# A four-layer trunk on one core: the first S5 recurrence in a written order on all engines, with its phases in the first step and its operators built on VectorE

## The chip, the core and the metric

The kernel runs on one core of one Trainium2 chip. A core has a matrix engine (TensorE, "PE" in the profile, its weight loads "PEld"), a vector engine (VectorE, "DVE"), a scalar engine for activations (ScalarE, "ACT"), a general engine (GpSimd, "POOL") and a sync engine that issues DMAs (SyncE, "SP"). Each engine runs its own instructions in their order; semaphores tie the engines together. The metric is the device time of one launch in microseconds (us), lower is better. Before the change it is 2361.99 us, the median of three runs (2357.68 to 2366.71).

## What is computed

The reference runs 512 tokens of width 1024 through four layers: S5, gated linear attention, differential attention, S5; each mixer is followed by a SwiGLU block. Only the first S5 mixer matters here. Cut down, it is

```python
h = rmsnorm(x, norm_mix[0])
dt = exp(log_dt);  ab = exp((lam_re + 1j * lam_im) * dt)   # 64 groups x 64 states
bb = (ab - 1) / lam * b                                    # 64 states x 16 channels for each group
s[t] = ab * s[t - 1] + bb @ h[t]                           # for each group, 512 tokens
y = real(c @ s) + d_skip * h
z = gelu(y)
a, g = split(z @ w_glu);  x = x + a * sigmoid(g)
```

All arithmetic is in float32; large products use three passes with operands split into a rounded high part and a rest.

## The kernel before

The mixer takes four tokens at a time: 128 blocks of four tokens, and 64 groups as 32 pairs, so that a pair of groups fills 128 partitions (2 x 64 states, or 2 x 4 x 16 inputs). Eight steps kk = 0 to 7 each treat four pairs, that is 128 channels. Two steps share one "half" h = kk // 2 of eight pairs, for which the operators are made together.

For one step the work is as follows; the names are those of `s5_pipe` (L1267) and `s5_first` (L1397).

- `up` (L1295, L1303): PE turns four 128x128 tiles of the normed input `hu` (it lies in the tile `scr`), and ACT copies them to `room`, the step's input U.
- `states` (L1305): PE forms V, two banks of 128x512, as input operator (`in`) times U (L1311). DVE turns V by the phases `cs` (cosine and sine) with four products into `mods` (L1313 to L1316); an addition and a subtraction follow (L1318, L1319), on POOL in the first S5 and on DVE in the second one.
- `scans` (L1321): two scans along time on DVE with the decay `r4` (L1328, L1330), then four products with `cs` into `prods` (L1329, L1331 to L1333).
- `outputs` (L1335): PE sums U times `map` and the four `prods` times `out` into the bank `y` (L1340, L1342), ACT applies gelu (L1344).
- `turned` (L1350): PE turns the result back (`zp`, L1353); ACT rounds it into `zT` (L488) and DVE takes the rest (L489).
- `glu` (L1358): 12 products of 128x512 into four banks `acc` (L370 to L372), the second half of the GLU's columns. Their weights come by `staged` (L334, the tile `wst`), `high` (ACT, L346) and `low` (DVE, L350).

The first S5 also makes its operators while it runs (`steps` and `ins` in `s5_first`):

- X (the input operator's powers): `s5_x` with twelve DVE products and sums of `cross` (L1017 to L1019) for each half, in two parts of 9 and 3; `s5_xt` turns X on PE (`xps`, L1143), ACT copies it in (L1153).
- Q (the output operator's powers): `s5_qt` turns C on PE (`cps`, L1057), ACT places it (L1075), and six products and sums of 128x512 follow (L1017 to L1019 with tile Q), all on POOL.
- the map of four tokens onto four: `s5_rows` on PE (`rps`, L1110), DVE and ACT put it into `rsb` (L1120, L1124), and `s5_map` sends it through DRAM: one DMA out (L1126) and eight in (L1135).
- pads: DMAs copy Q into `out` and X's base into `bpad` (L1100).
- phases: `s5_phases_first` (L980) forms the phase of 128 time blocks with two small products (`rough`, L987, L988), takes whole turns off on ACT (L990, L992), forms the angle with three products (L994 to L996), clips it on DVE (L998), and takes sine, absolute value and cosine on ACT (L999 to L1001). It is called once per step, one step ahead, and fills the decay (L1003, L1004) as well.

Before all this stand `s5_small`, a long chain of DVE instructions on 128x64 tiles that makes decay, phase and scale out of the parameters, and `s5_in`, which normalizes x: squares on ACT (L470), the power -1/2 on POOL (L459), and scale and gain for two tiles on ACT and POOL (L477, L479) and for two on DVE (L481).

In this region the order of all five engines' instructions is what a scheduler makes of the program. The loop is laid out one step deeper than the data needs: step kk's turn runs `states(kk)`, `scans(kk-1)`, `outputs(kk-2)`, `turned(kk-2)`, `glu(kk-3)`. After the pipeline, `s5_glu` runs the rest of the GLU: the gates of the finished columns on ACT (L1548), then three more sets of 96 products of 128x512.

Of the kernel before, what the change touches and what calls it, by code (L numbers as in the profile page):

```python
# [11 lines left out]
F32 = mybir.dt.float32  # L12
# [256 lines left out]
class Trunk:  # L269
# [558 lines left out]
    def sincos(self, pool, sn, cs, r, n, tag):  # L828
# [6 lines left out]
        with self.tc.high_priority(offset=60):  # L835
            nc.scalar.activation(sn, r, AF.Sin)
            nc.scalar.activation(cs, a[:], AF.Sin, scale=-1.0, bias=self.halfpi[:])


    def s5_small(self, pool):  # L840
# [6 lines left out]
        nc.scalar.activation(warm[:], self.halfpi[:], AF.Sin)  # L847
        self.magic = cp.tile([P, 1], F32, name="magic")
# [5 lines left out]
        if True:  # L854
# [5 lines left out]
            draw = p.tile([16, P], F32, name="draw")  # L860
            nc.sync.dma_start(draw[:], i["s5_d"].rearrange("l (k p) -> (l k) p", p=P))
# [6 lines left out]
            nc.tensor.transpose(ps[:, 3, :16], draw[:], self.ident[:16, :16])  # L868
# [10 lines left out]
            v.tensor_copy(self.dcol[:], ps[:, 3, :16])  # L879
# [58 lines left out]
        p = Slices(self.wp.tile([P, 2048], F32, tag="whl", name="params2", bufs=5))  # L938
        self.s5_rows_of_phases(p, pool, keep["fhi"], keep["flo"], keep["f"])
# [3 lines left out]
    def s5_rows_of_phases(self, p, cp, fhi, flo, f):  # L943
# [4 lines left out]
        v = nc.vector  # L948
        part = p.tile([P, 96], F32, name="rowparts").rearrange("p (k z b) -> p k z b", z=3, b=4)
# [6 lines left out]
        nc.scalar.copy(hi[:], lo)  # L956
        v.tensor_copy(rest, hi[:].bitcast(F32))
        v.tensor_tensor(lo, lo, rest, op=ALU.subtract)
        self.frow = cp.tile([12, 8, P], F32R, name="frow")
        for q in range(2):  # L960
            ps = self.tp("frow")
            for j in range(4):
                nc.tensor.transpose(ps[:12, j], part[:, 4 * q + j].rearrange("p z b -> p (z b)"), self.ident[:])
            nc.scalar.copy(self.frow[:, 4 * q : 4 * q + 4], ps[:12])
# [9 lines left out]
        nc.scalar.mul(self.nident[:], self.ident[:], -1.0)  # L974
# [3 lines left out]
    def s5_phases_first(self, pool, kk, cs, r4):  # L978


        nc = self.nc
        mm = nc.tensor.matmul
        flat = lambda y: y[:].rearrange("p a b -> p (a b)")
        row = self.frow[:, kk]
        fine, rest = (self.counts[:, z].rearrange("p a b -> p (a b)") for z in range(2))
        rough = flat(self.tp("rough"))
        mm(rough, row, fine, start=True, stop=False)  # L987
        mm(rough, row, rest, start=False, stop=True)  # L988
        k = pool.tile([P, 512], F32, tag="turns", name="turns")
        nc.scalar.activation(k[:], rough, AF.Identity, bias=self.magic[:])  # L990
        kr = pool.tile([P, 512], F32R, tag="turnsr", name="turnsr")
        nc.scalar.activation(kr[:], k[:], AF.Identity, bias=self.mmagic[:])  # L992
        g = flat(self.tp("angle"))
        mm(g, row, fine, start=True, stop=False)  # L994
        mm(g, self.nident[:], kr[:], start=False, stop=False)
        mm(g, row, rest, start=False, stop=True)  # L996
        ca = k[:]
        nc.vector.tensor_scalar(ca, g, -0.5, 0.5, op0=ALU.max, op1=ALU.min)  # L998
        nc.scalar.activation(cs[:, 1], ca, AF.Sin, scale=self.two_pi)  # L999
        nc.scalar.activation(ca, ca, AF.Abs)  # L1000
        nc.scalar.activation(cs[:, 0], ca, AF.Sin, scale=-self.two_pi, bias=self.halfpi[:])  # L1001
        r4 = r4.rearrange("p (b m) -> p b m", m=P)
        nc.scalar.copy(r4, self.k5["r4"][:, 4 * kk : 4 * kk + 4].unsqueeze(2).broadcast_to([P, 4, P]))  # L1003
        nc.gpsimd.memset(r4[:, :, 0:1], 0.0)  # L1004
# [1188 lines left out]
```

## Time and profile before

| quantity | us |
|---|---|
| median of three runs | 2361.99 |
| the profiled execution, its own time | 2366.1 |
| span of the profile, first to last instruction | 2364.4 |
| PE busy in the span | 2245.8 (95%) |
| DVE, ACT, POOL busy in the span | 1586.0, 1119.2, 332.3 |
| first DVE instruction of the recurrence (L1313) | at 48.63 |
| first GLU gate behind the recurrence (L1548) | at 201.68 |

A row of the page's timeline gives start, duration, engine, line, operation, output<-input, shape and count, and in brackets how long the engine stood idle before it and whose completion ended the wait. A row of the group view gives count, total and mean time, and the idle time before. A row of the windows view gives, for one stretch, the busy time of every engine with its number of instructions, the granted TensorE clock (1.00 is full), the share of time that the DMA engines were busy, and GB/s. Successive instructions of one engine overlap a little, so the distance from start to start is shorter than the duration.

### The profile page before, as it was taken

The numbers are of one execution on the slowest core, as the hardware profiler recorded it, in microseconds if no ns is written. First come the engines' busy times: TensorE is split into PE (matmuls) and PEld (weight loads), VectorE is DVE, ScalarE is ACT, GpSimd is POOL, SyncE is SP. The second block draws the span as 40 slices with busy tenths as digits, with TensorE's granted clock in tenths as the row PEclk, the third lists the DMA queues.
The fourth block names the chain that finished last, engine by engine and source line by source line (L and its number), as shares of the span: only waits on it lengthen the run. The fifth ranks groups of instructions, "written<-read, shape, count | busy, mean of one in ns | idle before, by whom it ended". The sixth has DMA issues, their size and how long they took to land. (4 is left out here: it accounts for less than half of the span.)

```text
span 2364.4 us, 37216 instructions
## 1 busy us (share of the span) xinstructions
PE 2245.8 (95%) x14847; PEld 1985.6 (84%) x14847; DVE 1586.0 (67%) x2416; ACT 1119.2 (47%) x1790; POOL 332.3 (14%) x417
## 2 busy tenths in 40 slices
PE   4799989999999999999999998999999799999997
PEld 3577888898977789898987787989999688989996
DVE  7765587876833468786753566886856864967674
ACT  3454454554552346555544575653534233634442
POOL 3330123324000011111001231111000100101000
PEclk9699999999999999999999999999999899999999
DMA  4114676676332268576344564895742545766631
GB/s 111 32 39 142 160 186 155 165 178 156 86 104 72 79 144 212 146 181 177 108 140 116 115 134 122 209 240 127 187 98 81 121 130 151 176 175 157 162 77 67
DMA packets 291719, 320.17 MB, mean 135 GB/s; under 512 B 68005, under 2 KB 231097, under 8 KB 291290
## 3 DMA queue, kind: packets, MB, share of 16 engines
q1 hardware_dynamic: 229434, 236.57, 33.4%
q0 software_dynamic: 62112, 81.22, 18.7%
q8 instruction: 117, 1.92, 0.3%
q14 instruction: 56, 0.46, 0.1%
HBM read 285.88 MB, written 16.65 MB: 128 GB/s over the span
## 5 line engine op out<-in xcount | busy, mean ns | idle before, releaser
L350 DVE TENSOR_TENSOR whl<-wst,whl 128x1024 fp32r<-128x1024 f32 x272 | 332.1, 1223 | 310.2 <-ACT whl L346 309.6
L346 ACT CAST whl<-wst 128x1024 fp32r<-128x1024 f32 x272 | 285.2, 1050 | 383.2 <-PE acc L372 265.5
L535 PE MATMUL a<-side,whl 128*128 128x256 f32 x3168 | 388.7, 280 | 9.0 <-ACT whl L346 5.9
L535 PEld LDWEIGHTS a<-side,whl 128*128 128x128 f32 x3168 | 375.9, 191 | 11.0 <-ACT whl L346 7.1
L370 PE MATMUL acc<-whl,act 128*128 128x512 f32 x704 | 278.2, 395 | 3.0 <-DVE g L580 3.0
L371 PE MATMUL acc<-whl,act 128*128 128x512 f32 x704 | 275.0, 391 | 0.0
L372 PE MATMUL acc<-whl,act 128*128 128x512 f32 x704 | 274.7, 390 | 0.0
L535 PE MATMUL c<-side,whl 128*128 128x256 f32 x2112 | 255.8, 278 | 4.3 <-DVE whl L350 4.3
L535 PEld LDWEIGHTS c<-side,whl 128*128 128x128 f32 x2112 | 248.6, 189 | 4.7 <-DVE whl L350 4.7
L350 DVE TENSOR_TENSOR whl<-slot,whl 128x1024 fp32r<-128x1024 f32 x105 | 127.9, 1223 | 66.4 <-ACT whl L346 65.9
L370 PEld LDWEIGHTS acc<-whl,act 128*128 128x128 f32 x704 | 132.1, 188 | 33.2 <-DVE g L580 4.2
L372 PEld LDWEIGHTS acc<-whl,act 128*128 128x128 f32 x704 | 132.2, 188 | 28.0
L371 PEld LDWEIGHTS acc<-whl,act 128*128 128x128 f32 x704 | 132.2, 188 | 25.9 <-issue 0.2
L370 PE MATMUL acc<-whl,hT 128*128 128x512 f32 x352 | 143.4, 407 | 2.1 <-DVE ro L1918 1.5
L346 ACT CAST whl<-slot 128x1024 fp32r<-128x1024 f32 x105 | 110.0, 1052 | 73.9 <-PE acc L372 28.2
L371 PE MATMUL acc<-whl,hT 128*128 128x512 f32 x352 | 138.4, 393 | 1.0 <-DVE whl L350 1.0
L372 PE MATMUL acc<-whl,hT 128*128 128x512 f32 x352 | 138.5, 394 | 0.0
L535 PE MATMUL a<-sides,whl 128*128 128x256 f32 x1056 | 134.0, 283 | 1.6 <-DVE x L518 1.6
L535 PE MATMUL d<-sides,whl 128*128 128x256 f32 x1056 | 133.5, 283 | 1.3 <-ACT whl L346 1.3
L535 PEld LDWEIGHTS a<-sides,whl 128*128 128x128 f32 x1056 | 129.4, 191 | 2.7 <-issue 2.0
L535 PEld LDWEIGHTS d<-sides,whl 128*128 128x128 f32 x1056 | 128.9, 191 | 2.0 <-ACT whl L346 1.9
L571 POOL DMA_DIRECT2D wst<-in_ffn_w_gate_up_dram x44 | 56.8, 1290 | 445.7 <-DMA wst<-in_ffn_w_gate_up_dram 257.1
(442 smaller groups left out, 3994.7 us busy)
## 6 DMA issues: line engine op xcount, KB each, us to landing
wst<-in_ffn_w_gate_up_dram SPq DMA_DIRECT2D x88, 512.0 KB, 4.5
wst<-in_ffn_w_down_dram SPq DMA_DIRECT2D x88, 512.0 KB, 4.6
slot<-in_ffn_w_gate_up_dram SPq DMA_DIRECT2D x69, 512.0 KB, 5.4
wst<-in_ffn_w_gate_up_dram POOLq DMA_DIRECT2D x44, 512.0 KB, 6.3
halves<-in_ffn_w_gate_up_dram SPq DMA_DIRECT2D x42, 512.0 KB, 6.2
wst<-in_s_w_glu_dram SPq DMA_DIRECT2D x32, 512.0 KB, 3.9
wst<-in_gla_w_in_dram SPq DMA_DIRECT2D x24, 512.0 KB, 3.7
wst<-in_diff_w_qkv_dram SPq DMA_DIRECT2D x24, 512.0 KB, 3.8
```

The lines of the kernel that those rows point to most:

```text
L346: self.last["high"] = self.nc.scalar.copy(hl[:, 0], w[:])
L350: self.last["low"] = self.nc.vector.tensor_tensor(hl[:, 1], w[:], hl[:, 0].bitcast(F32), op=ALU.subtract)
L370: mm(out, lh, rh, start=first, stop=False)
L371: mm(out, lh, rl, start=False, stop=False)
L372: self.last["mm"] = mm(out, ll, rh, start=False, stop=last)
L535: mm(o, hl[:, x, k, c], side[:, y, k], start=first and not (j or k or n), stop=k == 3 and n == 2, skip_group_check=True,)
L571: nc.gpsimd.dma_start(w[:], left.quarter(*plus, b), accum_op=ALU.add)
```

## The change

The change rewrites the order of the first S5 by hand and moves some of its work.

1. `s5_pipe` gets `before` and `hooks`. With hooks, all five engines take the program's order as written (`hand_all`), and the loop is one step shallower: `states(kk)`, `outputs(kk-1)`, `up(kk+2)`, `products(kk+1)`, `turned(kk-1)`, scans and turns of kk, `rest(kk-1)`, `glu(kk-2)`. `products` (the PE part of the former `states`) is now one step ahead of the DVE part; `split_t` is taken apart into `turned` (ACT) and `rest` (DVE).
2. The addition and the subtraction in `states` run on DVE in both S5.
3. Q is made by DVE instead of POOL: in odd steps Q, in even steps X. X's first part is split into a base (`pre`) and `one`.
4. Phases are made early: those of steps 0 and 1 ahead of or in the start, 2 to 5 started in step 0, 6 and 7 in step 1 (sines in step 3). Their banks come from `acc` instead of `tp`; `cs` gets five places, the decay its own tile (`s5_decays`).
5. The input gain goes into the input operator: `bb` is multiplied by the gain, laid out by group with two DMAs, instead of x; d_skip gets the gain as well. `s5_in` then only scales by ACT; the eps is added on ACT too. The input operator has two buffers, and one `xps` bank holds both its parts.
6. The GLU's weights are fetched once per even step at its end, rounded (ACT) at the start of the next even step, and the rest is taken (DVE) right behind its `states`.
7. In the start, the two sine instructions on ACT come ahead of the squares of x (`issue_after`).

The core of the diff:

```diff
+        if hooks:
+            hook = lambda name, kk: hooks[name](kk) if name in hooks else None
+            self.hand_all()
+            before(up, products)
+            for kk in range(10):
+                hook("first", kk)
+                if kk % 2 == 0 and kk:
+                    hls[kk // 2 - 1] = self.high(stage[kk // 2 - 1], 2, 512)
+                hook("operators", kk)
+                if kk < 8:
+                    states(kk)
+                if kk % 2 == 0 and kk:
+                    self.low(hls[kk // 2 - 1], stage[kk // 2 - 1])
+                hook("behind states", kk)
+                if 1 <= kk < 9:
+                    outputs(kk - 1)
+                if kk + 2 < 8:
+                    up(kk + 2)
+                if kk + 1 < 8:
+                    products(kk + 1)
+                hook("behind products", kk)
+                if 1 <= kk < 9:
+                    turned(kk - 1)
+                hook("behind zp", kk)
+                if kk < 8:
+                    scan(kk, 0)
+                    scan(kk, 1)
+                    hook("behind scans", kk)
+                    for k in range(4):
+                        turn(kk, k)
+                hook("beside", kk)
+                if 1 <= kk < 9:
+                    rest(kk - 1)
+                hook("beside 2", kk)
+                if kk % 2 == 0 and kk < 8:
+                    stage[kk // 2] = self.staged(self.wb_src(wg, kk, D), 2, 512)
+                if kk >= 2:
+                    glu(kk - 2)
+                hook("last", kk)
+            self.hand()
+            return accs
...
+            def before(up, products):
+                phases((0, "rough"))
+                up(0)
+                ins(0)
+                phases((0, "angle"), (0, "clip"), (0, "sines"))
+                new_x(1)
+                products(0)
+                phases((1, "rough"))
+                decays(0)
+                up(1)
+                phases((1, "angle"))
+                out_pads(0)
+                out_pads(1)
+                raw[2] = self.s5_loads(p, 0, 16, 8, 2)
...
+            def operators(kk):
+                if kk + 1 < 8:
+                    ins(kk + 1)
+                    decays(kk + 1)
+                if kk % 2 and kk < 7:
+                    new_q(kk // 2 + 1)
+                if kk % 2 == 0 and kk < 8:
+                    rv[kk // 2] = self.s5_rows(8, bp, Q[kk // 2][0])
...
+            def behind_products(kk):
+                if kk == 0:
+                    phases((1, "clip"), (2, "rough"), (1, "sines"))
+                    rows[1]()
+                    phases((2, "angle"), (3, "rough"))
+                if kk % 2 == 0 and 2 <= kk < 7:
+                    out_pads(kk + 1)
...
+            def behind_scans(kk):
+                if kk == 0:
+                    phases((2, "clip"), (2, "sines"), (3, "angle"))
...
+            def beside(kk):
                 h = kk // 2
+                if kk == 0:
+                    X[1][2]()
+                    phases((3, "clip"), (4, "rough"), (3, "sines"), (4, "angle"))
+                elif kk % 2 == 0 and h + 1 < 4:
+                    new_x(h + 1)
+                elif kk % 2 and kk < 7:
+                    Q[h + 1][2]()
+
+            def beside_2(kk):
+                h = kk // 2
+                if kk % 2 == 0 and kk < 6:
+                    if kk:
                         X[h + 1][2]()
+                    X[h + 1][3]()
+                    self.s5_b_pads(bp, X[h + 1][0])
+                if kk == 0:
+                    phases((4, "clip"), (5, "rough"), (4, "sines"), (5, "angle"))
+                if kk == 1:
+                    phases((6, "rough"), (6, "angle"), (6, "clip"), (7, "rough"))
+                if kk % 2 and kk < 7:
+                    Q[h + 1][3]()
+                    out_pads(kk + 1)
...
+        def pre():
+            if gain is not None:
+                g = gain[:, b0 : b0 + nb].unsqueeze(1).broadcast_to([P, 2, nb, 16])
+                eng.tensor_tensor(bb[:], bb[:], g, op=ALU.mult)
             f(0, 0, X[:, 0, :, 0], bb[:, 0], bb[:, 1], ALU.subtract)
             f(0, 0, X[:, 1, :, 0], bb[:, 1], bb[:, 0], ALU.add)
```

In step 1, `behind_states` clips and takes the sines of step 5; in step 2, `first` forms the angle of step 7 and `behind_states` clips it and starts the map (as in each even step); in step 3, `behind_zp` takes the sines of steps 6 and 7. From the end of the recurrence on, each engine's instructions are the same as before and in the same order.

More of the change, by code (lines that the diff above doesn't have):

```diff
@@ L993, in s5_phases_first @@
[L993 to L1001, printed above, removed]
@@ L1002, in s5_phases_first, with rough @@
-        r4 = r4.rearrange("p (b m) -> p b m", m=P)
-        nc.scalar.copy(r4, self.k5["r4"][:, 4 * kk : 4 * kk + 4].unsqueeze(2).broadcast_to([P, 4, P]))
-        nc.gpsimd.memset(r4[:, :, 0:1], 0.0)
+        k = self.np_.tile([P, 512], F32, tag="h", name="turns")
+        at = {}
+        def rough():
+            p = self.acc("rough")[:]
+            mm(p, row, fine, start=True, stop=False)
+            mm(p, row, rest, start=False, stop=True)
+            nc.scalar.activation(k[:], p, AF.Identity, bias=self.magic[:])
+            at["kr"] = kr = self.np_.tile([P, 512], F32R, tag="hh", name="turnsr", bufs=2)
+            nc.scalar.activation(kr[:], k[:], AF.Identity, bias=self.mmagic[:])
@@ L1474, in s5_first @@
+            rv = {}
+            hooks = {
+                "first": first, "operators": operators, "behind states": behind_states, "behind zp": behind_zp,
+                "behind products": behind_products, "behind scans": behind_scans, "beside": beside, "beside 2": beside_2,
+            }
+            accs = self.s5_pipe(0, hu, zT, True, room, get, before, hooks)
         self.x = self.xp.tile([P, NT, D], F32, tag="x", name="x")
```

317 lines of the change are left out of this document (196 added, 121 removed).

## The prediction

> **What bounds the kernel now.** I read the windows first, cut at the two ends of the recurrence, then the groups of POOL and DVE inside it, then the same recurrence in the second S5 as a timeline.
>
> ```profile
> 48.60:201.70 153.10, 131.26 (x1019) 105.31 (x1019) 102.82 (x134) 75.15 (x125) 51.50 (x45) 0.83 0.24 52
> 201.70:272.20 70.50, 70.50 (x326) 58.27 (x324) 29.36 (x36) 25.01 (x40) 5.12 (x4) 1.00 0.62 171
> ...
> 201.68 2.67 ACT L1548 ACTIVATE gate<-acc 128x512 f32<-128x512 f32 x4 [1.82 <-PE acc L372]
> ```
>
> The columns are PE, PEld, DVE, ACT, POOL busy, then the granted clock. From 201.7 on PE is busy 70.50 of 70.50 us at full clock, and its later order is unchanged, so whatever the change gains must be gained before that gate. In the 153.1 us before it no engine is full: DVE 102.8, ACT 75.2, POOL 51.5, PE 131.3 at a mean clock of 0.83. That is about 131.3 x 0.83 = 109 us of full-clock work, 13.6 a step, in steps that take 153.1/8 = 19.1. The engines wait for each other.
>
> ```profile
> L1319 POOL TENSOR_TENSOR mods<-mods 128x512 f32<-128x512 f32 x8 | 14.6, 1820 | 2.4 <-DVE mods L1316 2.4
> L1019 POOL TENSOR_TENSOR Q<-Q,dq 128x512 f32<-128x512 f32 x8 | 12.2, 1524 | 0.3
> ...
> L1328 DVE TENSOR_TENSOR_SCAN mods<-cs,mods 128x512 f32<-128x512 f32 x8 | 12.6, 1573 | 1.2 <-POOL mods L1318 1.2
> ```
>
> A POOL pass over 128x512 takes 1.5 to 1.8 us, and the scan on DVE beside it 1.57 in the mean. The second S5 has no such POOL work:
>
> ```profile
> 1904.70 0.69 DVE L1313 TENSOR_TENSOR mods<-V,cs 128x512 f32<-128x512 f32 x1
> ...
> 1908.29 1.23 DVE L1328 TENSOR_TENSOR_SCAN mods<-cs,mods 128x512 f32<-128x512 f32 x1
> ...
> 1910.54 0.67 DVE L1329 TENSOR_TENSOR prods<-mods,cs 128x508 f32<-128x508 f32 x1
> ...
> 1912.91 0.69 DVE L489 TENSOR_TENSOR zT<-zp,zT 128x512 fp32r<-128x512 f32 x1
> 1914.12 1.23 DVE L350 TENSOR_TENSOR whl<-wst,whl 128x1024 fp32r<-128x1024 f32 x1 [0.51 <-ACT whl L346]
> 1915.26 0.68 DVE L1313 TENSOR_TENSOR mods<-V,cs 128x512 f32<-128x512 f32 x1
> ```
>
> Here a scan is 1.2, and DVE runs without gaps: six passes for `states` in 1908.29 - 1904.70 = 3.59, two scans in 2.25, four turns in 2.37, low 1.14. A plain pass is 0.60 from start to start. These are the prices of the written order.
>
> **The start.** In before, six rows set it:
>
> ```profile
> 16.10 1.06 ACT L470 ACTIVATE sq<-xin 128x1024 f32<-128x1024 f32 x1 [8.82 <-DMA xin<-in_x_dram]
> 17.28 0.15 DVE L457 TENSOR_SCALAR ms<-ms 128x1 f32<-128x1 f32 x1 [1.99 <-ACT sq L470]
> 18.58 1.13 ACT L477 ACTIVATE sq<-xin,rs 128x1024 f32<-128x1024 f32 x1
> 19.89 2.34 DVE L904 TENSOR_TENSOR params<-params 128x64 f32<-128x64 f32 x1
> ...
> 46.48 3.75 PE L1311 MATMUL V<-room 128*128 128x128 f32 x16 [0.24 <-ACT room L1303]
> ...
> 48.63 0.69 DVE L1313 TENSOR_TENSOR mods<-V,cs 128x512 f32<-128x512 f32 x1 [4.18 <-PE V L1311]
> ```
>
> DVE's parameter chain loses 2.0 us at 17.28 and 2.1 at 19.89 (a 0.2 us instruction that took 2.34 beside POOL's gain product); both causes go. The gain product on `bb` and the split of `dcol` add about 1. So X of half 0 is ready some 3 us earlier. The normed input no longer passes through DVE and POOL: from x's arrival (16.1; the gain's two DMAs of 64-byte pieces now lie ahead of it, I take 16.8) ACT does four squares, four small additions, four scalings, two small copies: 4 x 1.25 + 4 x 0.2 + 4 x 1.13 + 0.8 = 11.1, done at 28.0. Then `rough`, `up`, `xps`, `angle` and V follow on PE at the slow rate of the 46.48 row (3.75 for V), back to back from 28.4 to 37.3, with clip and sines beside V. `states(0)` starts at about 36.7: 12 us ahead of 48.63.
>
> **Steps 0 and 1.** What is added here is the phases of steps 2 to 7. ACT carries them:
>
> ```profile
> L1001 ACT ACTIVATE cs<-turns,halfpi 128x512 f32<-128x512 f32 x8 | 5.8, 723 | 0.1
> L992 ACT ACTIVATE turnsr<-turns,mmagic 128x512 fp32r<-128x512 f32 x8 | 5.8, 722 | 0.3
> L990 ACT ACTIVATE turns<-rough,magic 128x512 f32<-128x512 f32 x8 | 5.5, 687 | 3.1 <-PE rough L988 2.7
> ...
> L999 ACT ACTIVATE cs<-turns 128x512 f32<-128x512 f32 x8 | 5.0, 631 | 7.0 <-DVE turns L998 7.0
> L1000 ACT ACTIVATE turns<-turns 128x512 f32<-128x512 f32 x8 | 5.0, 628 | 0.0
> ...
> 41.34 0.80 PE L995 MATMUL angle<-turnsr,nident 128*128 128x512 f32 x1
> 42.06 0.79 PE L996 MATMUL angle<-counts,frow 12*128 12x512 f32 x1
> ```
>
> A phase costs ACT 1.4 for the turns and 2.0 for the sines, and PE five products of 0.72 at the slow rate, half of that at full clock. Queued on ACT in step 0: the turns of step 1, seven copies of about 0.6, four times 3.4, in all 19.5. That gives 56 if PE always delivers; at full clock the `rough`-after-`angle` chain adds 4 (60.5), at half clock 11 (67.7). In step 1 the path to `states(2)` runs over y(0) on PE, gelu, V, `zp` and the copy to `zT` on ACT, `rest(0)` on DVE, the turns and angle of step 6, its clip, and the second half of Q, because DVE's order puts them in that row: 15 us at full clock (PE 8, five ACT passes 4, DVE 3), about 21 at half. So `states(2)` starts between 75.5 and 88.3. I take 84: the phases' products, of which four in five use 12 of 128 rows, are what PE does in step 0, so the clock will mostly be low. So the head start is spent here, on phases that before still had to make in its later steps.
>
> **Steps 2 to 7** are then bound by DVE. Its other prices:
>
> ```profile
> 28.08 0.55 DVE L1017 TENSOR_TENSOR X<-X,pw 128x384 f32<-128x384 f32 x1
> 28.55 0.55 DVE L1019 TENSOR_TENSOR X<-X,dx 128x384 f32<-128x384 f32 x1
> ...
> 92.64 0.28 DVE L1018 TENSOR_TENSOR dx<-bb,s5fi 128x128 f32<-128x128 f32 x1
> 92.84 0.28 DVE L1017 TENSOR_TENSOR X<-bb,s5fr 128x128 f32<-128x128 f32 x1
> ...
> 166.08 0.36 DVE L1120 SCALAR_TENSOR_TENSOR rsb<-mask,dcol,rps 128x16 f32<-128x16 f32 x2
> ...
> 183.21 1.07 DVE L489 TENSOR_TENSOR zT<-zp,zT 128x512 fp32r<-128x512 f32 x1
> 184.19 2.35 DVE L350 TENSOR_TENSOR whl<-wst,whl 128x1024 fp32r<-128x1024 f32 x2
> ```
>
> Q's six passes on DVE are not in the trace: 0.47 for 128x384 here is the low end, POOL's 1.5 the high one. I take 0.60, the plain pass of the same size. Gain 0.33, base 6 x 0.2, X 6 x 0.47, rest 1.0. An even step: 3.6 + 1.14 + 0.36 + 2.25 + 2.37 + 1.53 + 1.0 + 2.82 = 15.1 (step 2 has one clip more, 15.7; step 6 has no X, 10.7). An odd step: 3.6 + 2.25 + 2.37 + 1.0 + 3.6 = 12.8. Steps 2 to 6 are 15.7 + 12.8 + 15.1 + 12.8 + 10.7 = 67.1. PE's 13.6 a step falls to about 12 without the phases and lies beside it, if at full clock; ACT has 5 to 6. The new waits of the written order: on DVE `rest(kk-1)` stands ahead of the second part of X or Q and waits for ACT's copy to `zT`, whose chain (y 4.5, gelu, V, `zp`, copy) ends 9 to 10 us into a step at full clock, while DVE gets there at 10 to 12; with PE at half clock it is some 6 late, and then X or Q, `rps`, the map and the next y are late with it. On PE `rps` waits for the end of Q with y behind it; y ends there 5.4 into the step, early enough. On SP the GLU's weights and the next norm's gain (it waits for zp(6)) queue behind pads and maps; they are needed 11 and 22 us later and cost nothing while the queue runs. The decay's own tile, the joint `xps` bank and the eps on ACT lie under DVE's row and cost nothing either; uncovered they would cost their ACT time, under 1 us a step.
>
> **The tail.** y(6) needs the last map, made in step 6 at 5.2 and sent through DRAM:
>
> ```profile
> 132.84 0.57 SPq L1126 DMA_DIRECT2D rd<-rsb  x1
> 134.87 3.65 SPq L1135 DMA_DIRECT2D scr<-rd  x8
> ...
> scr<-rd SPq DMA_DIRECT2D x32, 32.0 KB, 2.0
> ...
> 166.68 0.38 PE L1340 MATMUL y<-scr,room 128*128 128x128 f32 x2
> 171.14 1.95 PE L1311 MATMUL V<-room 128*128 128x128 f32 x16
> ```
>
> From DVE's row to landing: 0.6 to the issue, 2.0, 3.7 for eight issues on SP, 2.0: 8.3. So y(6) starts at 13.5 of step 6, 2.8 into step 7. Behind it in PE's order: y 4.5, gelu and `zp` 1.5, glu(5) 2.7, y(7) 4.5, gelu and `zp` 1.4, glu(6) and glu(7) 2.7 each: 22.8 after the start of step 7. (y is 171.14 - 166.68 = 4.46; twelve GLU products are at most 70.50/24 = 2.9 by the second window, which holds three sets of 96 and some transposes.)
>
> **The clock.** Three windows of 3.4 us in before:
>
> ```profile
> 142.40:145.80 3.40, 3.40 (x9) 2.08 (x9) 3.40 (x3) 2.95 (x5) 1.85 (x1) 0.61 0.00 1
> 145.80:149.20 3.40, 3.40 (x13) 2.52 (x12) 1.34 (x2) 0.38 (x2) 0.00 (x0) 0.50 0.02 5
> 149.20:152.60 3.40, 3.40 (x17) 3.40 (x17) 0.00 (x0) 3.35 (x5) 0.10 (x1) 0.50 0.00 0
> ```
>
> PE was busy throughout, and the clock stayed at half for three windows. One such episode costs PE 5 us, of which about 2 fit into a step's slack: I add one, 3. The Trainium skill's page "TensorE: Matmul & The Clock Gate" (Part 1: The HAM clock gate) says that the full clock comes back after about one busy window of 3.4 us; these rows disagree. By it the low clock would be short, `states(2)` would start near 75.5, and the time would be the third rival's.
>
> **The sum.** 84 + 67.1 + 22.8 + 3 = 177 for the end of glu(7). In before it lies 2.0 behind the first gate, at 203.7. The gain is 26.7, and the profiled execution's 2366.1 becomes 2339.4. The median of the runs shown is 4.1 below that execution: 2335.
>
> **The rivals.** (1) Slower: the half clock holds through the DVE-bound steps, because each leaves PE gaps of 2 to 3 us. A step is then PE's, 2 x 12 = 24 instead of 14. Steps 2 to 7 and the tail from 88.3: 88.3 + 5 x 24 + 2 x 19 = 246, 43 us later than before: 2405. It decides from about three such steps on (3 x 10 eats the 27). For it: 0.50 in the rows above; against it: those spells ended while PE was dense, and a PE-bound step is dense. 5%. (2) The phases do not overlap: turns, angle, clip and sines run in turn, 1.4 + 1.5 + 0.7 + 2.0 + 1.3 = 6.9 for each of five. `states(2)` starts near 99, the end is 192, the gain 11: 2350, no change that can be told. For it: PE and ACT pass every phase to and fro twice; against: the order puts another phase's sines into each wait. 9%. (3) PE at full clock from step 0 on and no episode: 75.5 + 67.1 + 22.8 = 165.4, gain 38: 2324. 20%. (4) DVE's new passes cost more: Q at 1.05 (between its bounds) is 24 x 0.45 = 11 more, or SP's map chain is late by 3 in each even step: 2345. 13%. The forecast keeps 53%.
>
> **How the numbers follow.** About 0.5%, 12 us, is what a measurement of this kernel can tell from no change. Forecast, (3) and (4) are faster, 86%; (2) and the edge of (4) same, 8%; (1) and the unforeseen slower, 6%. The range runs from (3) with a start 8 us better to rival (2): 2316 to 2351.
>
> **What would show it.** `states(0)` near 37; ACT nearly full between 40 and 62; a distance of two steps near 28 from step 2 on, with DVE above 9 tenths; no POOL pass over 128x512; the first gate near 175. Wrong would be a granted clock of 0.5 over several of the later steps, or DVE waiting for PE's V or ACT's zT there.

## The result and the profile after

The changed kernel takes 2345.73 us (median of 5 runs, 2341.71 to 2348.9) where the kernel before takes 2359.25 (5 runs, 2355.8 to 2366.71): a ratio of 0.9938, 95% interval 0.9916 to 0.9959. That is 13.5 us less, half of what was forecast. The forecast went from 2361.99, the median of the three runs known then; with five runs the median of before is 2.7 lower. The profiled execution of the changed kernel has an own time of 2344.99 and a span of 2343.3.

In the new kernel's lines the six passes of `states` are L1384 to L1389, the scans L1393, the turns L1402 and L1406, `y` L1413 and L1415, gelu L1417, `zp` L1430, ACT's copy to `zT` L1431 and DVE's rest L1435. The map's rows are L1156 and L1160, its DMAs L1162 and L1171. The weights' load is L336, their rounding and low part L346 and L350 as before, the reload of x L1689, the gate L1763. Where an experiment adds lines, the later numbers shift by as many.

First the busy row of the page after:

```profile
PE 2234.0 (95%) x14847; PEld 1981.7 (85%) x14847; DVE 1594.0 (68%) x2461; ACT 1114.6 (48%) x1769; POOL 275.6 (12%) x378
```

POOL has lost 57 us and DVE gained only 8. Next the windows of after, cut at the starts of steps 0, 1, 2 and 7 on DVE and at the first gate, with steps 3 and 6 singly, and then the same cut of before; the columns are those of the forecast.

```profile
36.35:57.90 21.55, 16.94 (x118) 11.02 (x116) 14.18 (x26) 15.22 (x25) 0.21 (x2) 0.75 0.39 75
57.90:78.45 20.55, 16.79 (x125) 13.08 (x123) 14.38 (x23) 14.48 (x24) 0.10 (x1) 0.75 0.04 8
78.45:153.99 75.54, 67.04 (x666) 60.19 (x666) 68.41 (x115) 31.07 (x51) 0.53 (x5) 0.91 0.24 50
...
96.37:109.92 13.55, 13.15 (x142) 11.85 (x142) 13.08 (x21) 7.89 (x14) 0.11 (x1) 1.00 0.21 52
...
143.36:153.99 10.63, 10.20 (x103) 9.39 (x102) 10.63 (x18) 3.61 (x6) 0.11 (x1) 1.00 0.14 29
153.99:182.73 28.74, 21.21 (x118) 19.13 (x118) 16.30 (x20) 8.02 (x10) 0.97 (x1) 0.82 0.75 253
```

```profile
48.63:172.30 123.67, 105.25 (x838) 82.36 (x838) 83.52 (x113) 64.41 (x112) 47.58 (x42) 0.79 0.19 37
172.30:201.68 29.38, 25.96 (x184) 22.91 (x183) 19.30 (x21) 10.72 (x13) 3.89 (x3) 1.00 0.47 119
```

The first gate comes 201.68 - 182.73 = 19.0 us earlier. Of these, 48.63 - 36.35 = 12.3 are the earlier start, 123.67 - (21.55 + 20.55 + 75.54) = 6.0 come from the way from `states(0)` to `states(7)`, and the tail, 28.74 against 29.38, gives almost nothing.

Most of the earlier start is the normed input. Its last tile came from DVE in before, behind a power on POOL (first row), and comes from ACT now (second row):

```profile
35.69 1.28 DVE L481 SCALAR_TENSOR_TENSOR scr<-xin,rs,gain 128x1024 f32<-128x1024 f32 x1 [0.46 <-POOL rs L459]
```

```profile
26.64 1.15 ACT L1318 ACTIVATE scr<-xin,rs 128x1024 f32<-128x1024 f32 x1
```

It is ready 9.2 us earlier (27.8 instead of 37.0), and the chain from there to `states(0)` takes 8.6 instead of 11.7. No run puts a part of the start back alone, so the 12.3 are read from the two traces, and what each of its parts is worth stays open.

Behind the gate nothing has changed; the second set of gates serves below as the mark for it:

```profile
182.73 2.59 ACT L1763 ACTIVATE gate<-acc 128x512 f32<-128x512 f32 x4 [3.54 <-PE acc L372]
...
228.19 2.64 ACT L1763 ACTIVATE gate<-acc 128x512 f32<-128x512 f32 x4 [2.34 <-PE acc L372]
```

In before it stands at 247.23, 19.04 later. From there to the end of the span it is 2117.2 us in before and 2115.1 after, and between 2113.8 and 2120.5 in the experiments below, which all have the same instructions there. So one execution's time says less about this change than the place of that mark, and the 21.1 us between the two profiled executions are more than the 13.5 between the medians.

Three things make the new steps and the tail longer than the forecast had them. The first is what DVE waits for, by the timeline of DVE (all rows with a wait from step 1 to step 7):

```profile
73.15 1.08 DVE L1435 TENSOR_TENSOR zT<-zp,zT 128x512 fp32r<-128x512 f32 x1 [4.42 <-ACT zT L1431]
75.91 0.69 DVE L1016 TENSOR_SCALAR turns<-angle 128x512 f32<-128x512 f32 x1 [1.68 <-PE angle L1013]
92.32 1.08 DVE L1435 TENSOR_TENSOR zT<-zp,zT 128x512 fp32r<-128x512 f32 x1 [1.63 <-ACT zT L1431]
107.00 1.08 DVE L1435 TENSOR_TENSOR zT<-zp,zT 128x512 fp32r<-128x512 f32 x1 [0.41 <-ACT zT L1431]
124.52 1.09 DVE L1435 TENSOR_TENSOR zT<-zp,zT 128x512 fp32r<-128x512 f32 x1 [2.96 <-ACT zT L1431]
140.46 1.06 DVE L1435 TENSOR_TENSOR zT<-zp,zT 128x512 fp32r<-128x512 f32 x1 [1.65 <-ACT zT L1431]
```

In each of steps 1 to 5 DVE arrives at `rest(kk-1)` before ACT has made the high part: 6.65 us in steps 2 to 5. From the start of gelu to the end of the copy it is 3.7 us in each of these four steps; what differs is when y(kk-1) ends, 10.1, 6.9, 10.8 and 8.1 us into the step. In step 4 the sines of steps 6 and 7, written in step 3, run on ACT ahead of the copies of the input operator (`inm`), and PE waits for these with y(3). Here are ACT's timeline (the six passes of the sines, from 108.28 to 112.27, left out) and a row of PE's:

```profile
106.99 1.28 ACT L1020 ACT_TABLE_LOAD   x1
...
112.18 1.03 ACT L346 CAST whl<-wst 128x1024 fp32r<-128x1024 f32 x1
113.11 1.18 ACT L1203 COPY inm<-xps 64x512 f32<-64x512 f32 x2
```

```profile
114.35 0.49 PE L1413 MATMUL y<-scr,room 128*128 128x128 f32 x2 [3.61 <-ACT inm L1203]
```

After this wait y(3) takes 6.4 us, with a clock of 0.55 between 115.20 and 118.60. In step 2 the clock is 0.50 from 77.80 to 84.60, and y(1) starts 4.4 us into the step.

The second and third are in the tail; here are the timelines of SP, ACT and PE, one after the other.

```profile
148.89 0.38 SPq L1162 DMA_DIRECT2D rd<-rsb  x1
152.41 3.64 SPq L1171 DMA_DIRECT2D scr<-rd  x8
...
158.79 1.65 SPq L336 DMA_DIRECT2D wst<-in_s_w_glu_dram  x3
166.61 0.35 SPq L450 DMA_DIRECT2D gain<-in_norm_ffn_dram  x1
169.96 28.36 SPq L336 DMA_DIRECT2D wst<-in_s_w_glu_dram  x8
```

```profile
167.46 2.96 ACT L346 CAST whl<-wst 128x1024 fp32r<-128x1024 f32 x3
175.34 1.05 ACT L346 CAST whl<-wst 128x1024 fp32r<-128x1024 f32 x1 [4.92 <-DMA wst<-in_s_w_glu_dram]
176.29 0.59 ACT L1417 ACTIVATE z<-y 128x512 f32<-128x512 f32 x1
```

```profile
157.83 0.77 PE L1413 MATMUL y<-scr,room 128*128 128x128 f32 x2 [3.62 <-DMA scr<-rd]
158.39 1.92 PE L1415 MATMUL y<-scr,prods 128*128 128x128 f32 x8
...
164.09 1.06 PE L1415 MATMUL y<-scr,prods 128*128 128x128 f32 x8
...
176.94 1.11 PE L1430 MATMUL zp<-ident,z 128*128 128x128 f32 x4 [3.15 <-ACT z L1417]
```

y(6) waits 3.62 us for the last map, and after that idle time a quarter of it takes 1.92 instead of 1.06 (the clock is 0.50 from 159.40 to 162.80). On ACT four roundings of the gate's weights stand ahead of gelu(7). The fourth waits 4.92 us for a load that SP can issue only at 169.96, when a `low` has freed one of the three buffers, and with it wait gelu(7), `zp(7)` and PE.

### The profile page after: what moved, and what is told of

Same layout as the page of the kernel before. It is cut to its first block, busy times and chain, and to the rows that moved or that the text cites. A ratio compares the mean times of both kernels' runs of the same rounds, so it can differ in the third digit from the quotient of the medians.

```text
span 2343.3 us, 37163 instructions
## 1 busy us (share of the span) xinstructions
PE 2234.0 (95%) x14847; PEld 1981.7 (85%) x14847; DVE 1594.0 (68%) x2461; ACT 1114.6 (48%) x1769; POOL 275.6 (12%) x378
## 3 DMA queue, kind: packets, MB, share of 16 engines
q8 instruction: 117, 1.92, 0.3%
## 5 line engine op out<-in xcount | busy, mean ns | idle before, releaser
L350 DVE TENSOR_TENSOR whl<-wst,whl 128x1024 fp32r<-128x1024 f32 x272 | 332.1, 1223 | 304.5 <-ACT whl L346 303.9
L346 ACT CAST whl<-wst 128x1024 fp32r<-128x1024 f32 x272 | 285.6, 1052 | 384.2 <-PE acc L372 267.3
L350 DVE TENSOR_TENSOR whl<-slot,whl 128x1024 fp32r<-128x1024 f32 x105 | 127.9, 1223 | 65.8 <-ACT whl L346 65.7
L346 ACT CAST whl<-slot 128x1024 fp32r<-128x1024 f32 x105 | 110.2, 1054 | 73.8 <-PE acc L372 28.1
```

The costliest lines, as they stand in the source:

```text
L346: self.last["high"] = self.nc.scalar.copy(hl[:, 0], w[:])
L350: self.last["low"] = self.nc.vector.tensor_tensor(hl[:, 1], w[:], hl[:, 0].bitcast(F32), op=ALU.subtract)
```

## The experiments

Each kernel is the changed one with one edit, unless more is said. "Second set" is the second set of gates; "behind step 7" is its distance from DVE's first pass of `states(7)`, 228.19 - 153.99 = 74.20 in the changed kernel.

**The rounding behind the tail.**

```diff
+            self.last_zt = nc.scalar.copy(dst(kk)[0], zp[:])
+            self.last_rest = v.tensor_tensor(d[1], zps[kk][:], d[0].bitcast(F32), op=ALU.subtract)
...
+        with self.tc.issue_after(self.last_zt.ins), self.tc.issue_after(self.last_rest.ins):
             return self.s5_glu(0, zT, accs, i["norm_ffn"][0])
```

> Edit: the rounding of the gate's GLU weights on ACT stands behind the last copy to zT, and its low part on DVE behind the last rest; nothing else moves. Theory A (the order on ACT costs the tail): gelu(7) starts right behind y(7), 2.6 us earlier than the 176.3 of the changed kernel, PE's 3.15 us of idle time ahead of zp(7) shrinks to about 0.7, and the first gate stands near 180 instead of 182.7: 2 to 3 us less. Rival B (the weights themselves come too late, by their load of 5.3 us): the gate comes earlier, but PE then waits for the split of the next weights between 183 and 200, and the time stays within 1 us.

```profile
175.98 0.60 ACT L1417 ACTIVATE z<-y 128x512 f32<-128x512 f32 x1 [5.34 <-PE y L1415]
...
181.04 2.33 ACT L1764 ACTIVATE gate<-acc 128x512 f32<-128x512 f32 x4
184.61 1.05 ACT L346 CAST whl<-wst 128x1024 fp32r<-128x1024 f32 x1 [1.24 <-DMA wst<-in_s_w_glu_dram]
```

On ACT's timeline gelu(7) now waits for y(7) alone. This execution reached step 7 at 155.88, 1.9 later than the changed kernel's, so distances count: first gate 25.16 instead of 28.74 behind step 7, second set (226.26) 70.38 instead of 74.20. ACT now waits for weights behind the gate, but PE loses nothing by it (45.2 us from the first set to the second, 45.5 in the changed kernel). Median 2340.19 (ratio 0.991, 0.9893 to 0.9927). Theory A holds: the order on ACT cost 3.8 us. Of these, 2.2 lie ahead of gelu(7) (20.1 instead of 22.3 behind step 7); the rest lies behind it, where `zp(7)` takes 0.66 instead of 1.11.

**The reload of x, first try.** A memset over z(7), which waits for `zp(7)`, is written ahead of the reload:

```diff
             accs = self.s5_pipe(0, hu, zT, True, room, get, before, hooks)
+            nc.gpsimd.memset(room[5][:, 0:4], 0.0)
```

> Edit: a 4-column memset on POOL over z(7), which waits for zp(7), stands ahead of the reload of x, so that the 2 MB move after 177 instead of from 162.6. Theory C (the loads of the GLU weights are late because the reload shares the DMA engines with them): the load before the fourth rounding falls from 5.3 to 3 to 4 us, gelu(7) starts 1.5 to 2.5 us earlier, the first gate near 180.5. Rival A (what is late is the order: the load can't be issued before a low has freed its buffer): gelu(7) moves by less than 1 us and the time by less than 1.

The reload still went out 8.61 us behind step 7 (164.60 - 155.99), as in the changed kernel (162.60 - 153.99): the memset came behind it in POOL's order. So nothing relevant changed, and the run tells nothing of theory C. It stands as a second measurement of the changed kernel: 2345.45 (4 runs, 2345.14 to 2346.57), second set 73.67 behind step 7. So two executions of the same order differ by 0.5 in this distance, and a difference from 74.20 of that size tells nothing.

**The last map first.**

```diff
                     rv[kk // 2] = self.s5_rows(8, bp, Q[kk // 2][0])
+                    if kk == 6:
+                        self.s5_map(0, 24, 8, rv[3], rs, mops[1])
...
-                if kk % 2 == 0 and kk < 8:
+                if kk % 2 == 0 and kk < 6:
```

> Edit: the last map's rows leave PSUM ahead of the states of step 6 instead of behind its low part; its DMAs go out about 3.5 us earlier. Theory D (the map's way through DRAM sets y(6)): DVE waits 0.8 us for rps at the start of step 6, rd goes out near 145.5 instead of 148.9, y(6) starts near 154.5 instead of 157.8, on a PE that has just finished glu(4), so that y takes 4.5 instead of 7.2 us; the first gate is 4 to 6 us earlier, near 178. Rival B (the weights' loads bound the tail): y(6) is as early, but gelu(7) still waits for the load and the gate is no more than 1.5 us earlier.

y(6) started 9.5 us into step 6 (155.71 - 146.23) instead of 14.5, at full clock. But on ACT:

```profile
175.61 1.04 ACT L346 CAST whl<-wst 128x1024 fp32r<-128x1024 f32 x1 [8.71 <-DMA wst<-in_s_w_glu_dram]
176.56 0.59 ACT L1417 ACTIVATE z<-y 128x512 f32<-128x512 f32 x1
```

The load was issued at 167.09, 2.9 earlier than in the changed kernel, and came no earlier, with the reload of x in flight from 165.20. The second set stands 72.53 behind step 7, 1.7 less; counted from step 5, so with DVE's wait for `rps`, it is 98.9 instead of 99.6. Median 2347.85, ratio 0.9931 (0.9917 to 0.9945). Rival B.

**PE fills its wait.**

```diff
+                if kk == 7:
+                    glu(5)
                 if 1 <= kk < 9:
                     outputs(kk - 1)
+                if kk == 8:
+                    glu(6)
...
-                if kk >= 2:
+                if kk >= 2 and kk not in (7, 8):
                     glu(kk - 2)
```

> Edit: on PE glu(5) stands ahead of y(6), and glu(6) ahead of zp(7); nothing else moves. Theory E (PE is idle while it waits for the map, and what it could do there lies behind): glu(5) fills 154.2 to 157, y(6) runs at full clock, 4.5 instead of 7.2 us, glu(6) lies beside gelu(7), and the first gate is 4 us earlier, near 179. Rival B (the weights' load holds gelu(7), whatever PE does before): the gate is 1 to 2 us earlier, for glu(6) alone.

y(6) ran at full clock right behind glu(5), and gelu(7) at 168.97. Then two roundings (ACT's timeline) held the copy to `zT`, and PE waited 6.88 us for that:

```profile
175.55 1.04 ACT L346 CAST whl<-wst 128x1024 fp32r<-128x1024 f32 x1 [5.98 <-DMA wst<-in_s_w_glu_dram]
176.88 1.04 ACT L346 CAST whl<-wst 128x1024 fp32r<-128x1024 f32 x1 [0.29 <-DMA wst<-in_s_w_glu_dram]
177.83 1.07 ACT L1431 CAST zT<-zp 128x512 fp32r<-128x512 f32 x1
```

The second set is 73.74 behind step 7, 0.5 less, no more than the scatter; median 2346.0, ratio 0.9925 (0.9909 to 0.9942). Again rival B: whatever comes earlier on PE waits for the same load.

**The reload of x, behind zp(7).**

```diff
+            late = nc.gpsimd.memset(room[5][:, 0:4], 0.0)
...
+        with self.tc.issue_after(late.ins):
             nc.gpsimd.dma_start(self.x[:], i["x"][0].rearrange("(t p) c -> p t c", p=P))
```

> Edit: the reload of x (2 MB) is put behind a 4-column memset on POOL that waits for zp(7), so it goes out near 177 instead of 162.6. Theory C (the weights' load that holds gelu(7) is late because it shares the DMA engines with the reload): the fourth load takes about 3 us instead of 5.3, lands before y(7) ends, gelu(7) starts within 0.7 us of the end of y(7), and the first gate stands 2 to 3 us earlier against step 7's start. Rival A (it is late because it can only be issued when a low has freed its buffer): gelu(7) still starts 2 us or more behind y(7).

The reload went out at 177.12. The load issued at 170.34 was split from 174.50 on, 4.2 us later, where the changed kernel took 5.4; gelu(7) started at 175.46; the second set is 73.12 behind step 7, 1.1 less. Median 2345.43, ratio 0.9932 (0.9917 to 0.9947). In the second measurement of the changed kernel the load took 4.7. The two theories share the wait: 0.5 to 1.2 us go with the reload beside the load, the rest is that the load can only be issued behind a `low`.

**The three together** (late reload, early map, PE fill).

> Edit: the late reload of x, the early map and the PE fill together. Theory (the three are in series: each alone only moves the wait to the weights' load): with the load out of the way the early map and the fill count now, the first gate comes 6 to 9 us earlier against step 7's start than the 28.7 of the changed kernel, so 20 to 23, and the second gate set near 221 instead of 228.2. Rival (the tail is bound by the buffers of the weights, not by the DMA): 26 or more.

First gate 176.11 - 152.98 = 23.1 behind step 7, second set at 222.90, 69.92 behind: 4.3 less, where the three alone gave 1.1, 1.7 and 0.5. PE still waited 4.74 us for the copy of zT(7), behind two roundings. Median 2341.8, ratio 0.9919 (0.9905 to 0.9933). That is 1.0 more than their sum, and a little short of what was expected (20 to 23, and 221). What speaks for a series is the wait itself: ACT waited 8.7 us for the load with the early map alone, 6.0 with the fill alone and 3.4 here.

**The rest behind the second part of X or Q.**

```diff
                 hook("beside", kk)
-                if 1 <= kk < 9:
-                    rest(kk - 1)
                 hook("beside 2", kk)
+                if 1 <= kk < 9:
+                    rest(kk - 1)
```

> Edit: rest(kk-1) on DVE stands behind the second part of X or Q instead of ahead of it; nothing else moves. Theory F (the steps are longer than predicted because DVE waits at rest for ACT's copy to zT): the waits at rest (4.4 in step 1, 1.6, 0.4, 3.0, 1.7 in steps 2 to 5) go, steps 2 to 6 take 69 instead of 75.5 us and the first gate comes 6 to 10 us earlier. Rival G (DVE waits there because PE and ACT are the ones that set the step): the wait goes to the next states (for PE's V) or to the operands of X and Q, and the five steps still take 74 or more.

```profile
79.57:149.92 70.35, 64.70 (x664) 59.37 (x664) 68.25 (x114) 30.38 (x50) 0.53 (x5) 0.91 0.28 55
```

This is the window of steps 2 to 6: 70.35 instead of 75.54, DVE busy 97%. In step 1 the wait only moved (7.18 us for the angle in place of 4.42 + 1.68). Step 7 starts 4.1 earlier, the second set (225.28) 2.9; the tail, bound by its load, gives 1.2 back. Median 2345.03, ratio 0.9929 (0.9913 to 0.9945): not told from the changed kernel by the times. Theory F for the steps; less than expected at the gate.

**Q's sums on POOL again.**

```diff
-                Q[h] = self.s5_q(nc.vector, p, 0, 8 * h, 8, 2)
+                Q[h] = self.s5_q(nc.gpsimd, p, 0, 8 * h, 8, 2)
```

> Edit: the cross sums of Q go back to POOL in their place of the written order (18 passes over 128x512 in odd steps), all else as changed. Theory H (taking Q off POOL was a gain, though DVE bounds the steps): six POOL passes of 1.5 us take 9 us of an odd step and slow DVE's scans beside them from 1.2 to 1.5; Q is late by 2 to 4 us for rps, the map and y, and three odd steps lose 6 to 12 us in all. Rival I (DVE's time is what counts): odd steps lose 3.6 us of DVE and the time falls by 5 or more.

Here is step 3 as a window, then from the timelines of DVE and POOL in it:

```profile
98.24:112.98 14.74, 12.94 (x140) 11.71 (x140) 14.74 (x14) 9.03 (x16) 9.91 (x7) 1.00 0.19 47
```

```profile
101.84 4.01 DVE L1393 TENSOR_TENSOR_SCAN mods<-r,mods 128x512 f32<-128x512 f32 x2
105.77 1.71 DVE L1406 TENSOR_TENSOR prods<-mods,cs 128x508 f32<-128x508 f32 x1
```

```profile
102.79 1.97 POOL L1045 TENSOR_TENSOR dq<-Q,pw 128x512 f32<-128x512 f32 x1
104.84 2.09 POOL L1046 TENSOR_TENSOR Q<-Q,dq 128x512 f32<-128x512 f32 x1
```

With 14 instructions instead of 21 DVE is busy longer, 14.74 against 13.08: two scans take 4.01 instead of 2.33, a turn 1.71 instead of 0.67. From step 1 to step 7 it is 96.19 us (155.86 - 59.67) against 96.09. Median 2345.91, ratio 0.9936 (0.9923 to 0.9949). Neither theory: what DVE is spared it loses by working beside POOL, and moving Q to DVE was worth nothing by itself.

**The addition and the subtraction on POOL again.**

```diff
-            v.tensor_tensor(m[:, 0], m[:, 0], m[:, 1], op=ALU.add)
-            v.tensor_tensor(m[:, 2], m[:, 2], m[:, 3], op=ALU.subtract)
+            w = nc.gpsimd if hooks else v
+            w.tensor_tensor(m[:, 0], m[:, 0], m[:, 1], op=ALU.add)
+            w.tensor_tensor(m[:, 2], m[:, 2], m[:, 3], op=ALU.subtract)
```

> Edit: the addition and the subtraction of states go back to POOL in their place of the written order, all else as changed. Theory M (this is where the steps were shortened): a POOL pass of 1.8 us between DVE's multiplications and its scan cannot be filled in the written order; each step gets about 1.6 us longer (2.4 + 1.8 + 1.8 + 1.4 against 3.6 + 2.25), less what DVE's wait at rest already holds (0.4 to 4.4 a step), so steps 2 to 6 take 79 to 83 instead of 75.5 us and the first gate comes 4 to 9 us later. Rival N (as with Q on POOL, what DVE is spared pays for what it waits): the five steps stay within 2 us of 75.5.

```profile
85.22 3.38 DVE L1394 TENSOR_TENSOR_SCAN mods<-r,mods 128x512 f32<-128x512 f32 x2 [1.79 <-POOL mods L1389]
```

Two scans take 3.38 beside POOL's subtraction and wait 1.79 before it, but the wait at `rest` is gone in steps 1 to 5, but for 0.49 in step 4: steps 2 to 6 take 75.98, the gate stands at 183.36, the second set at 228.90, 0.7 later. The median, 2348.72 (ratio 0.9952, 0.9939 to 0.9964), is 3.0 above the changed kernel's, with intervals that overlap. Rival N, by the trace.

**The phases spread over steps 0 to 5.** The pieces in the old places go; in step kk now stand those of step kk+2:

```diff
             def behind_products(kk):
                 if kk == 0:
+                    phases((1, "clip"), (1, "sines"))
                     rows[1]()
+                if kk + 2 < 8:
+                    phases((kk + 2, "rough"))
...
             def behind_zp(kk):
+                if kk + 2 < 8:
+                    phases((kk + 2, "angle"))
...
             def beside(kk):
+                if kk + 2 < 8:
+                    phases((kk + 2, "clip"), (kk + 2, "sines"))
...
-            p = self.acc("rough")[:]
+            p = (self.acc if kk < 2 else self.tp)("rough")[:]
```

(The bank of `angle` changes in the same way.)

> Edit: the phases of steps 2 to 7 are made two steps ahead, one in each of steps 0 to 5, instead of most of them in steps 0 and 1; their rough and angle banks come from the transposes' two, since the accumulators hold the GLU from step 2 on. Theory J (the head start is spent on early phases, and it is a wash): states(2) starts near 68 instead of 78.5, steps 2 to 5 each get 2 to 3 us longer (3.4 us on ACT and two table loads of 1.28 ahead of the zT copy, five products on PE, the banks), and the first gate stands within 3 us of 182.7. Rival K (early phases pay): states(2) gains less than 5, the later steps lose 4 or more each, the first gate comes 8 us or more later.

From DVE's timeline:

```profile
65.04 0.69 DVE L1021 TENSOR_SCALAR turns<-angle 128x512 f32<-128x512 f32 x1 [5.58 <-PE angle L1018]
...
105.13 0.69 DVE L1021 TENSOR_SCALAR turns<-angle 128x512 f32<-128x512 f32 x1 [6.36 <-PE angle L1018]
...
142.84 0.69 DVE L1021 TENSOR_SCALAR turns<-angle 128x512 f32<-128x512 f32 x1 [6.24 <-PE angle L1018]
```

`states(2)` starts at 70.48, 8 us earlier, but DVE then waits for an angle in every step, and steps 2 to 5 take 77.86 instead of 64.91, 3.2 more each in the mean, most of it in steps 3 and 5 (20 us each). The gate is at 187.69 and the second set at 233.17, both 5.0 later; median 2353.99 (12 runs), ratio 0.9972 (0.9957 to 0.9987). Between the two theories: the early phases cost 7.7 us more in steps 0 and 1 and save 13.0 in steps 2 to 5, so they pay 5 us at the gate. This is the only part undone whose loss the trace shows clearly. What in it costs the time is not told apart: the wait for the angle in its new place, the banks shared with the transposes, or the rows ACT_TABLE_LOAD of 1.28 us on ACT, of which the recurrence has nine in before, three in the changed kernel and eleven here.

**Two versions that go further.** The three together with the rest moved, and then with the rounding behind the tail too.

> Edit: the late reload of x, the early map and the PE fill, and rest behind the second part of X or Q. Theory: the two gains are in different places and add up: steps 2 to 6 take 70 instead of 75.5, from the start of step 7 to the second gate set it takes 70 instead of 74.2, and that set stands 8 to 10 us earlier than the 228.2 of the changed kernel, near 219; the median is 8 us below the changed kernel's. Rival: the weights' load, which starts when a low has run and not with the step, holds the tail where it was; 224 or more.

> Edit: the one before, with the rounding of the gate's weights behind the last zT copy too. Theory A: zT(7) no longer waits behind two roundings (PE waited 4.74 us for it with the late reload, early map and fill), so 2 to 4 us more: the second gate set near 216. Rival B (the split that is put off is needed right after, and the reload of x then shares its time): PE waits for the weights behind the gate, and the second set is no earlier than without it.

With the rest: second set at 219.90, steps 2 to 6 in 71.14, 69.75 behind step 7; median 2338.52, ratio 0.991 (0.9895 to 0.9925). With the rounding as well, ACT's timeline:

```profile
170.01 2.61 ACT L1772 ACTIVATE gate<-acc 128x512 f32<-128x512 f32 x4
...
215.47 2.64 ACT L1772 ACTIVATE gate<-acc 128x512 f32<-128x512 f32 x4 [2.35 <-PE acc L372]
```

Both sets stand 12.7 us earlier than in the changed kernel: 3.1 by the start of step 7, and 9.6 behind it (the second set at 64.56 instead of 74.20). PE's longest wait in the tail is 1.1 us. Median 2333.15 (4 runs, 2332.25 to 2338.37), ratio 0.9891 (0.9875 to 0.9907): it beats both kernels, 12.6 below the changed one's median (11 by the two ratios), and the two intervals against before don't meet. Both came out as expected, except that the order on ACT gave 5.2 us in the tail (69.75 - 64.56) and not 2 to 4.

## Why the prediction was right, and where its size was off

The sign held and the time lies in the range, near its slow end; the gain was half the size. Taken apart at the first gate, the start gave 12.3 where 12 was forecast, the way from `states(0)` to `states(7)` 6.0 where 9.3 was, and the tail 0.6 where 5.6 was (8.6 less the 3 for the clock). So the mechanism held for the start, in part for the steps, and failed for the tail. By its steps:

- **What lies behind the gate is unchanged**: right, 2115.1 against 2117.2 us from the second set to the end.
- **The start**: `states(0)` at 36.35, forecast 36.7.
- **Steps 0 and 1**: `states(2)` at 78.45, between 75.5 and 88.3 but 5.5 ahead of the 84 that was taken. The clock came back sooner than assumed. In the windows of after it was 0.50 from 50.6 on while PE was busy 2.2 of 3.4 us, and 0.98 one window after the first full one:

```profile
57.40:60.80 3.40, 2.23 (x5) 0.90 (x3) 3.40 (x6) 2.73 (x6) 0.00 (x0) 0.50 0.01 2
60.80:64.20 3.40, 3.40 (x45) 3.02 (x46) 3.40 (x5) 1.81 (x3) 0.00 (x0) 0.50 0.03 7
64.20:67.60 3.40, 3.40 (x34) 3.23 (x31) 3.40 (x7) 3.21 (x9) 0.10 (x1) 0.98 0.00 0
```

  That is the rule which the forecast weighed and set aside: the Trainium skill, page "TensorE: Matmul & The Clock Gate", Part 1 (The HAM clock gate), has the full clock return after about one busy window of 3.4 us. These rows agree with it, the three full windows in before (0.61, 0.50, 0.50) do not. By the rule `states(2)` would have started near 75.5, and it came 3 later. The choice of 84 rested on products that use few rows holding the clock low; no run shows that, since in the stretch at 0.50 PE was also idle a third of the time. The 5.5 us hide most of the 8.4 that steps 2 to 6 took too long, and that is luck. (As written, ACT's queue in step 0 is 19.2 and not 19.5, and 67.7 + 21 is 88.7; neither matters.)
- **That the head start is spent on phases which before still had to make later**: right in kind. The price was 42.1 us for steps 0 and 1, where the sum had 47.3 (84 - 36.7); that it buys shorter steps later is shown by the kernel with spread phases, where steps 2 to 5 get 3.2 longer each.
- **The prices on DVE**: right. A pass is 0.60 from start to start (step 3 keeps DVE busy for 13.08 where 12.8 was forecast), Q included. But no time hung on it: with Q on POOL the way from step 1 to step 7 is the same within 0.1 us.
- **Steps 2 to 6**: 75.5 instead of 67.1. The failing step is the wait at `rest`, put at nothing because the chain to the copy "ends 9 to 10 us into a step at full clock, while DVE gets there at 10 to 12". DVE got there at 10.2 to 12.2, but the copy ended at 10.6 to 14.6, and DVE waited 6.65 in all in steps 2 to 5; with `rest` moved the five steps take 70.35. What is left there against 67.1 is DVE's own time, 68.25, and 2.1 of gaps, of which 1.6 still lie at `rest` (0.77 and 0.85, in steps 4 and 6). The chain was late at its head: y, which was to end "5.4 into the step, early enough" in the even steps, ended at 10.1 and 10.8, at half clock in step 2, and in step 4 behind the sines of steps 6 and 7, which "ACT has 5 to 6" did not weigh against the copies behind them.
- **The tail**: 22.8 us were forecast from step 7 to the end of glu(7), which in before lies 2.0 behind the gate; by that measure it took 30.7. For its length this is the term that was mis-sized most, and in four pieces: the map landed 1.0 later than forecast, because its way out to DRAM took 3.5 us from issue to the next issue instead of 2.0; y(6) took 7.4 instead of 4.5 on a PE that had been idle 3.6 us; gelu(7) stood 2.5 behind the end of y(7); and from gelu(7) on it took 8.4 instead of 6.8, as `zp(7)` (1.11 in its row) and glu(6) started at half clock. The sentence that failed is the one that let the GLU's weights "cost nothing while the queue runs": it looked at SP's queue and not at ACT's, where the rounding of weights yet to be loaded stands ahead of gelu(7).
- **One episode of the clock, 3 us**: there were several, but the costs are in the two items above. Counted singly, -5.5 + 8.4 + 7.9 - 3 makes the gate 7.8 later than forecast; the rest of the span was 2.1 shorter, and so the profiled execution came to 2345.0 and not 2339.4.
- **From the execution to the median**: the forecast took 4.1 off, as in before; after, the profiled execution lies 0.7 below the median. That is the other half of the 10.7 us between 2335 and 2345.73.

Of the signs that were named, `states(0)`, a DVE busy above 9 tenths in steps 2 to 6 (91%) and the missing POOL passes came. ACT was busy for only 16.2 of the 22 us from 40 to 62, two steps took 31.5 and 33.4 instead of 28, and the gate came at 182.73 instead of 175. One of the two signs of being wrong came too: DVE waited there for ACT's copy to `zT`.

Of the rivals, the slower one fell (steps 2 to 6 ran at a mean clock of 0.91), and phases that don't overlap fell with `states(2)` at 78 and not 99. The fourth rival gave the number, 2345, by another way: the map was late once, DVE's new passes not at all.

## What to carry to other kernels

A written order shows each engine's waits in place, so price the instruction that waits together with what stands behind it on its own engine: here a rounding for the next stage, which needed a load that needed a buffer, stood ahead of the last activation and cost 3.8 us, while three other improvements ahead of it were worth 0.5 to 1.7 alone and 4.3 together. Where several waits are in series, remove them together or judge each by the place of a mark in the trace, since the time moves little until the last one goes. And when an engine is relieved, ask what it waits for next: undoing Q's or the addition's move cost under 1 us in the trace, because DVE had been waiting there anyway or was slowed by its neighbour.

## What the runs showed that was not expected

- **DVE beside POOL.** DVE's passes over 128x512 get slower by up to 2.5 times while POOL works on tiles of that size (a turn 1.71 instead of 0.67, two scans 4.01 instead of 2.33), and POOL's passes are then 1.5 to 2.1 us long. The Trainium skill says on the page "Perfetto Trace Analysis" (Optimizing Scalar/DVE Operations) that the two share a read port, so that moving work between them might not help; the run with Q on POOL agrees, 96.19 against 96.09 us.
- **The length of step 0 varies by itself.** With the same instructions up to step 1 it took 19.9 us (56.00 - 36.07, the three together), 21.55 (the changed kernel) and 23.2 (59.65 - 36.42, the rounding behind the tail). The first spell of half clock falls earlier or later in it; what places it stays open.
